# Block 2's up projections as seven block products instead of eight

## The chip, the cores and the metric

The kernel runs on one core of a Trainium2 chip. The metric is the device time of one execution in microseconds (us); the median of three runs of the kernel before is 3358.54 us (3357.44 to 3358.71).

## The reference

The reference is two decoder stacks of depth 2 in float32, one behind the other, over 512 tokens of width 1024. Block 1 (with 16 meta tokens ahead, so 528) has a mixer and a convolved gated feed-forward in each layer. Block 2 has, in each of its two layers, a feed-forward, a mixer (differential attention in layer 0, a gated MLP in layer 1) and another feed-forward. The change is in the four feed-forwards of block 2:

```
def _swiglu_ffn(x, w_gate_up, w_down):
    g, u = jnp.split(x @ w_gate_up, 2, axis=-1)
    return (jax.nn.silu(g) * u) @ w_down

h = h + 0.5 * ffn(rmsnorm(h, g1))
h = h + mixer(rmsnorm(h, g))
h = h + 0.5 * ffn(rmsnorm(h, g2))
```

Here x is 512 x 1024, w_gate_up 1024 x 5632 (2816 gate and 2816 value columns) and w_down 2816 x 1024.

## The kernel before

Features lie on partitions and tokens in columns. A float32 product is made of three passes in the matrix type float32r: each operand is split into a high and a low part of 12 bits, and high x high, high x low and low x high are added in PSUM. So each 128 x 128 block of weights is met by three matmuls (function unit, all issued by the helper mm at L192), in block 2 of 512 columns, in block 1 of 264 or 258 columns (528 or 516 tokens in two PSUM banks). Every matmul instruction comes with a weight load of its own.

Weights come through class WStream in the order of their use. A unit is one column tile of an output, 128 x 1024 floats (512 KB). SP loads units ahead into three raw tiles (L110); each half of a unit (512 columns) is split by ScalarE, which copies it to whi (L124), and VectorE, which subtracts that from the raw half for wlo (L125). There are four buffers for split halves, so the split runs three halves ahead of the matmuls.

A feed-forward of block 2 (ffn2, L534) goes through 22 feature tiles in three groups (FGROUPS: 6, 8, 8). For each feature tile there is a gate unit and a value unit, each of 8 x 3 = 24 matmuls; VectorE multiplies each result by 1/rms (yg, yv, L161), ScalarE applies Silu, VectorE multiplies the two, and the product is split again into ghi (ScalarE, L186) and glo (VectorE). The down units of a group come behind the second tile of the next group: for each of the 8 tiles of the stream h one unit of 6 or 8 tiles x 3 matmuls of 512 columns, whose result VectorE adds to h (L170). In the last group each finished h tile is prepared at once for the next projection (prep: xhi on ScalarE, xlo on VectorE, a square and a sum of squares); the norm itself (finish_norm, L291) is computed behind the first unit that follows and multiplies results later, since each token's 1/rms commutes with the product.

The order of instructions on each engine is not the order in which this file writes them: a planner in the compiler, with its own costs, orders each engine's queue, and each engine then works through its queue in that fixed order. Slots and semaphores follow from the tiles' uses. In block 2 GpSimd (POOL) has no work but one memset; SP's queue holds the weight loads, in order.

Of the kernel before, what the change touches and what calls it, by code (L numbers as in the profile page):

```python
# [21 lines left out]
# tokens that the last convolution of block 1 reads, in two even parts  # L22
# [7 lines left out]
FGROUPS = ((0, 6), (6, 14), (14, 22))  # L30
LEVELS = (1, 2, 4, 8, 16, 32, 64)
# [7 lines left out]
# w_in column tiles of block 1 in the order they are worked on  # L39
# [45 lines left out]
class WStream:  # L85
    """Weight units in the order of their use: loaded ahead, then split exactly into two parts of 12 bits, by halves."""

    RAW = 3
    SPLIT = 4
    HALF = 4 * P  # L90

    def __init__(self, nc, pool):
        self.nc, self.pool = nc, pool
        self.items, self.halves = [], []
        self.raw, self.sp = {}, {}
        self.n_dma = self.n_split = self.i = 0

    def add(self, key, ap):
        n = ap.shape[1]
        for a in range(0, n, self.HALF):  # L100
            self.halves.append((len(self.items), a, min(n, a + self.HALF)))
        self.items.append((key, ap, len(self.halves)))

    def _dma(self, upto):
        while self.n_dma < min(upto, len(self.items)):
            ap = self.items[self.n_dma][1]
            t = self.pool.tile([P, 2 * self.HALF], F32, tag="raw", name="wraw", bufs=self.RAW)
            n = ap.shape[1]
            for a, b in ((0, n),) if self.n_dma else ((0, self.HALF), (self.HALF, n)):
                self.nc.sync.dma_start(t[:, a:b], ap[:, a:b])  # L110
            self.raw[self.n_dma] = t
            self.n_dma += 1

    def prime(self, n):
        self._dma(n)

    def _split(self, upto):
        while self.n_split < min(upto, len(self.halves)):
            u, a, b = self.halves[self.n_split]
            self._dma(u + self.RAW)  # L120
            t, n = self.raw[u], b - a
            hi = self.pool.tile([P, self.HALF], F32R, tag="hi", name="whi", bufs=self.SPLIT)
            lo = self.pool.tile([P, self.HALF], F32R, tag="lo", name="wlo", bufs=self.SPLIT)
            self.nc.scalar.activation(out=hi[:, 0:n], in_=t[:, a:b], func=AF.Copy)  # L124
            self.nc.vector.tensor_tensor(lo[:, 0:n], t[:, a:b], hi[:, 0:n].bitcast(F32), ALU.subtract)  # L125
            self.sp[self.n_split] = (hi, lo, n // P)
            self.n_split += 1

    def prepare(self, n):
        self._split(n)  # L130

    def get(self, key):
        """the parts (hi, lo, slabs) of the next unit, one after the other"""
        u = self.halves[self.i][0]
        k, _, end = self.items[u]
        assert k == key, (k, key)
        while self.i < end:
            i = self.i
            self.i += 1
            self._split(i + self.SPLIT - 1)  # L140
            yield self.sp.pop(i)


class Model:
    def __init__(self, tc, io):
        assert set(self.MERGE) == set(range(KD))
        self.tc, self.nc, self.io = tc, tc.nc, io
        self.pending_norm = None
        self.later = []
        self.slabwise = False  # L150
        self.budget = 0.0
        self.table, self.table_load, self.table_users = None, None, []

# [18 lines left out]
    def after(self, later, earlier):  # L172
        """issue order on one engine"""
# [4 lines left out]
    def act(self, out, a, f, **k):  # L178
        """activations keep to the order of their tables, so that a table is loaded once for all that use it in a row"""
# [14 lines left out]
    def split_scaled(self, src, gcol, hi, lo):  # L194
        """hi + lo = src * gcol"""
# [8 lines left out]
    def unit(self, key, x, new=None, ps=None, first=True, final=True):  # L204
        """psum of w^T x over the slabs of a unit, in three passes"""
# [3 lines left out]
        k, last = 0, self.ws.items[self.ws.halves[self.ws.i][0]][1].shape[1] // P - 1  # L209
# [26 lines left out]
    def new_g2(self):  # L236
        """a unit of block 1 in two tiles of the other kind, for when they have nothing else to do"""
        return self.new_s(), self.new_s()

    def new_s(self):  # L240
        return self.psum.tile([P, 512], F32, tag="s", name="s", bufs=4)

    def hv(self, k):
        """the tokens that the present block works on"""
# [24 lines left out]

    def xg(self, k):  # L270
# [25 lines left out]
    def means(self, parts, ones, src):  # L296
        """means over partitions, of both parts that src is split into"""
# [1161 lines left out]
```

## Time and profile before

| what | before |
|---|---|
| median of 3 runs | 3358.54 us |
| profiled execution: span from its first to its last instruction | 3354.3 us |
| runs' median less that span | 4.2 us |
| TensorE (PE) busy | 3335.8 us, 99% |
| weight loads (PEld) busy | 2894.8 us, 86% |
| VectorE (DVE) busy | 1891.4 us, 56% |
| ScalarE (ACT) busy | 1440.1 us, 43% |
| GpSimd (POOL) busy | 15.8 us |
| DMA | 298.24 MB, mean 89 GB/s |

The profiled execution has no time of its own beside its span. A row "A <-B" of a wait says that A sat idle until B was done. PE's busy time is modelled from the starts of pipelined matmuls, so rates are read here from counts in a stretch.

### The profile page before, as it was taken

To read this page: it belongs to the slowest core of one execution; us is meant where nothing else is said; L and a number is where in the kernel's file an instruction comes from. 1 tells how busy PE (TensorE), PEld (TensorE's weight loads), DVE (VectorE), ACT (ScalarE), POOL (GpSimd) and SP (SyncE) were. 2 spreads that over 40 slices of the span, in tenths; PEclk is the share of its full clock that TensorE was granted. 3 is DMA by queue.
4 is the path that set the end of the run, shared out by engine and by line. 5 is a ranking of instruction groups with operands and counts; after the bars stand their busy time and mean duration, and the time that the engine had idled before them with its cause. 6 is when DMAs were issued, how large, how long until landed. Compare 5 with 4: busy or idle time off the path is not lost.

```text
span 3354.3 us, 48141 instructions
## 1 busy us (share of the span) xinstructions
PE 3335.8 (99%) x19462; PEld 2894.8 (86%) x19462; DVE 1891.4 (56%) x3412; ACT 1440.1 (43%) x2531; POOL 15.8 (0%) x41
## 2 busy tenths in 40 slices
PE   8999999999999999999999999999999999999999
PEld 8999999999999998888887778888888888888887
DVE  7766665667665756544446764445444546554443
ACT  5664343456643435332346642324332335343322
POOL 1000000000000000000000000000000000000000
PEclk9999999999999999999999999999999999999999
DMA  3122322322223233233322123333233332223332
GB/s 127 58 64 89 90 93 89 94 76 64 70 89 95 89 95 95 87 102 94 95 88 67 45 85 94 95 95 94 90 100 94 96 118 88 88 89 94 96 96 91
DMA packets 85647, 298.24 MB, mean 89 GB/s; under 512 B 9761, under 2 KB 9761, under 8 KB 85297
## 3 DMA queue, kind: packets, MB, share of 16 engines
q1 hardware_dynamic: 83664, 289.51, 28.0%
q8 instruction: 153, 2.51, 0.3%
q0 software_dynamic: 1328, 3.56, 0.3%
q10 hardware_dynamic: 432, 2.10, 0.2%
q14 instruction: 70, 0.57, 0.1%
HBM read 293.03 MB, written 2.10 MB: 88 GB/s over the span
## 4 chain that ended last, share of the span: by engine, by line
PE 97%; ACT 1%; DVE 1%; DMA 0%; issue 0%; SPq 0%; ACTq 0%
PE g L192 89%; PE s L192 8%; DMA wraw<-w_in 0%; PE s L1182 0%; PE s L1149 0%; ACT L182 0%; DVE am L1169 0%; ACT p L186 0%; PE s L772 0%; PE s L1215 0%; ACT whi L124 0%; DVE wlo L125 0%; PE s L831 0%; ACT rtmp L186 0%; DVE s L161 0%
## 5 line engine op out<-in xcount | busy, mean ns | idle before, releaser
L124 ACT ACTIVATE whi<-wraw 128x512 fp32r<-128x512 f32 x1112 | 691.6, 623 | 1533.8 <-PE g L192 1460.3
L125 DVE TENSOR_TENSOR wlo<-wraw,whi 128x512 fp32r<-128x512 f32 x1112 | 749.2, 675 | 545.6 <-ACT whi L124 523.4
L192 PE MATMUL g<-xhi,whi 128*128 128x512 f32 (+2 forms) x3696 | 1052.6, 332 | 1.0 <-ACT whi L124 1.0
L192 PE MATMUL g<-xlo,whi 128*128 128x512 f32 (+2 forms) x3696 | 1047.1, 331 | 0.0
L192 PE MATMUL g<-xhi,wlo 128*128 128x512 f32 (+2 forms) x3696 | 1046.3, 331 | 0.2 <-DVE wlo L125 0.2
L192 PEld LDWEIGHTS g<-xhi,whi 128*128 128x128 f32 x3696 | 627.0, 189 | 72.6 <-ACT whi L124 1.2
L192 PEld LDWEIGHTS g<-xhi,wlo 128*128 128x128 f32 x3696 | 626.7, 189 | 65.9 <-DVE wlo L125 0.6
L192 PEld LDWEIGHTS g<-xlo,whi 128*128 128x128 f32 x3696 | 624.3, 189 | 66.7
L192 PE MATMUL g<-glo,whi 128*128 128x512 f32 (+1 forms) x1360 | 469.7, 366 | 0.1
L192 PE MATMUL g<-ghi,whi 128*128 128x512 f32 (+1 forms) x1360 | 469.8, 367 | 0.0
L192 PE MATMUL g<-ghi,wlo 128*128 128x512 f32 (+1 forms) x1360 | 469.7, 367 | 0.0
L192 PEld LDWEIGHTS g<-glo,whi 128*128 128x128 f32 x1360 | 244.0, 188 | 45.8 <-DVE glo L161 0.5
L192 PEld LDWEIGHTS g<-ghi,whi 128*128 128x128 f32 x1360 | 244.0, 188 | 45.3 <-ACT ghi L186 0.2
L192 PEld LDWEIGHTS g<-ghi,wlo 128*128 128x128 f32 x1360 | 243.8, 188 | 45.5
L161 DVE TENSOR_TENSOR yv<-g,rstd 128x512 f32<-128x512 f32 x88 | 60.9, 692 | 132.7 <-PE g L192 132.7
L170 DVE SCALAR_TENSOR_TENSOR h<-g,h 128x512 f32<-128x512 f32 x96 | 66.4, 692 | 120.6 <-PE g L192 120.6
L161 DVE TENSOR_TENSOR yg<-g,rstd 128x512 f32<-128x512 f32 x88 | 60.9, 692 | 130.0 <-PE g L192 129.9
L161 DVE TENSOR_TENSOR h<-g,h 128x512 f32<-128x512 f32 (+2 forms) x84 | 58.4, 697 | 92.8 <-PE g L192 92.8
L186 ACT ACTIVATE ghi<-yv 128x512 fp32r<-128x512 f32 x88 | 55.5, 631 | 121.4 <-DVE yv L161 121.4
L192 PE MATMUL g<-whi,xhi 128*128 128x512 f32 x256 | 102.6, 401 | 0.0
L192 PE MATMUL g<-whi,xlo 128*128 128x512 f32 x256 | 101.3, 396 | 0.0
L192 PE MATMUL g<-wlo,xhi 128*128 128x512 f32 x256 | 101.2, 397 | 0.0
(322 smaller groups left out, 3038.5 us busy)
## 6 DMA issues: line engine op xcount, KB each, us to landing
wraw<-w_up SPq DMA_DIRECT2D x88, 512.0 KB, 3.5
wraw<-w2a_up SPq DMA_DIRECT2D x88, 512.0 KB, 3.5
wraw<-w2b_up SPq DMA_DIRECT2D x88, 512.0 KB, 3.5
wraw<-w_in SPq DMA_DIRECT2D x51, 512.0 KB, 3.5
wraw<-w_down SPq DMA_DIRECT2D x32, 512.0 KB, 3.5
wraw<-w2a_down SPq DMA_DIRECT2D x32, 512.0 KB, 3.5
wraw<-w2b_down SPq DMA_DIRECT2D x32, 512.0 KB, 3.5
wraw<-wa_in SPq DMA_DIRECT2D x24, 512.0 KB, 3.5
```

The source lines that it names most:

```text
L124: self.nc.scalar.activation(out=hi[:, 0:n], in_=t[:, a:b], func=AF.Copy)
L125: self.nc.vector.tensor_tensor(lo[:, 0:n], t[:, a:b], hi[:, 0:n].bitcast(F32), ALU.subtract)
L161: self.nc.vector.tensor_tensor(out, a, b, op)
L170: self.nc.vector.scalar_tensor_tensor(out=out, in0=a, scalar=s, in1=b, op0=op0, op1=op1)
L186: i = self.nc.scalar.activation(out=out, in_=a, func=f, **k)
L192: self.nc.tensor.matmul(out, lhsT, rhs, start=start, stop=stop, **k)
```

## The change

The up projection of a feed-forward is cut into 11 pairs of feature tiles. For a pair, the weights are four blocks of 128 x 1024 floats: two feature tiles (f) by two halves of the 1024 inputs (h), each block holding gate and value side by side; the host lays them out so (_quads). The operand x is cut in four too: two halves of the inputs by two halves of the tokens (256 each). The 2 x 2 block product is formed with seven products of blocks instead of eight, in the form with seven sums of weight blocks and operands computed beforehand and the results combined afterwards. Each of the seven steps is 2 (gate, value) x 4 x 3 = 24 matmuls of 256 columns.

Seven weight blocks are split per pair (1024 columns at a time instead of 512). Four of them are sums. Two are made by DMA: SP loads one block, and GpSimd's queue then adds the second onto it in SBUF (accum_op). The other two are made by VectorE from raw tiles in place. There are 7 raw tiles and 4 buffers of split blocks during a feed-forward of block 2, and 3 and 2 otherwise.

Three PSUM chains of two banks (a, b, c) take the steps' results. ScalarE copies three intermediate results out (ev), VectorE subtracts them from later ones; the rest is as before (1/rms, Silu, product, split), with wider instructions. Down units of 6, 6, 6 and 4 tiles (PGROUPS) instead of 6, 8, 8; those of a group are interleaved with the steps of the next group's first pair, and two PSUM buffers are left for them.

Where a feed-forward follows, the h tiles are finished in the order 0, 4, 1, 5, ... (PAIRED), and prep_pair makes the sums and splits of the operand (prep_first for tiles 0 to 3, prep_second for 4 to 7). This holds for the end of block 1, the attention's and the gated MLP's output projections, and the last group of layer 0's second feed-forward; in front of a mixer prep is as before. Temporary tiles of the other stages are moved into tiles that the operand uses too.

```
+PGROUPS = ((0, 3), (3, 6), (6, 9), (9, 11))
...
+    def add_pair(self, key, quad, stage):
+        st = {}
+        def get(n, i):
+            if n not in st:
+                st[n] = self.item([quad[j] for j in i] if isinstance(i, tuple) else quad[i], stage)
+            return st[n]
+        def step(n):
+            k = key + (n,)
+            if n == 0:
+                self.part(k, get("11", 0), 1024, 0, (), True)
+            elif n == 1:
+                self.part(k, get("s", (1, 2)), 1024, 0, (), True)
+            elif n == 2:
+                self.part(k, st["11"], 1024, 0, ((st["11"], st["11"], st["s"]),), True)
+            elif n == 3:
+                self.part(k, get("12", 3), 1024, 0, (), True)
+            elif n == 4:
+                self.part(k, get("21", (1, 0)), 1024, 0, (), True)
+            elif n == 5:
+                self.part(k, st["12"], 1024, 0, ((st["12"], st["12"], st["11"]),), True)
+            else:
+                self.part(k, get("22", 2), 1024, 0, (), True)
+        return step
...
+            if isinstance(ap, list):
+                self.nc.sync.dma_start(self.raws[s], ap[0])
+                for b in ap[1:]:
+                    self.nc.gpsimd.dma_start(self.raws[s], b, accum_op=ALU.add)
+            else:
...
+        for o, x, y in sums:
+            self.nc.vector.tensor_tensor(self._tile(o), self._tile(x), self._tile(y), ALU.add)
+            for t in (o, x, y):
+                self._drop(t)
+        c = (hs[0] % 2) * self.HALF
+        hi = self.his[hs[0] // 2][:, c:c + n]
+        self.nc.scalar.activation(out=hi, in_=self._tile(src)[:, a:a + n], func=AF.Copy)
...
+    def _ahead(self):
+        while True:
+            more = self._hi()
+            while self.n_lo < self.n_hi and (not self.parts[self.n_lo][5] or self.n_lo < self.n_hi - 1):
+                self._lo()
+                more = True
+            if not more:
+                return
...
+    STEPS = ((0, "a", True), (1, "c", True), (4, "a", False), (2, "b", True), (5, "a", False), (3, "c", False),
+             (6, "a", False))
...
+    def prep_first(self, k, g, ng):
+        n = self.T // 2
+        a, b = self.hv(k)[:, 0:n], self.hv(k)[:, n:2 * n]
+        if k == 0:
+            self.tx = {}
+        self.tx[k] = [self.shared(3 * k + i, F32R) for i in range(3)]
+        self.dt = self.shared(12, name="dt")
+        d = self.dt[:, 0:n]
+        self.tt(d, a, b, ALU.subtract)
+        self.act(self.slot(k, 0), a, AF.Copy, scale=ng)
+        self.act(self.slot(k, 1), d, AF.Copy, scale=g)
+        self.stt(self.slot(k, 0, True), a, ng, self.slot(k, 0).bitcast(F32), ALU.mult, ALU.subtract)
+        self.stt(self.slot(k, 1, True), d, g, self.slot(k, 1).bitcast(F32), ALU.mult, ALU.subtract)
+    def prep_second(self, k, g1, g2):
+        n = self.T // 2
+        b1, h2, d, t4 = self.hv(k)[:, n:2 * n], self.hv(k + 4), self.dt[:, 0:n], self.dt[:, n:2 * n]
+        b2, t = (self.np.tile([P, T1], F32, tag=t, name="ops", bufs=1)[:, 0:2 * n] for t in ("nx", "nw"))
+        self.act(b2, h2, AF.Copy, scale=g2)
+        self.stt(t[:, 0:n], d, g1, b2[:, n:2 * n], ALU.mult, ALU.add)
+        self.stt(t[:, n:2 * n], b1, g1, b2[:, n:2 * n], ALU.mult, ALU.subtract)
+        self.tt(t4, b2[:, 0:n], t[:, 0:n], ALU.subtract)
+        for v, f in ((lambda lo: self.slots(k, 4, lo), t), (lambda lo: self.slots(k, 2, lo), b2), (lambda lo: self.slot(k, 6, lo), t4)):
+            self.act(v(False), f, AF.Copy)
+        for v, f in ((lambda lo: self.slots(k, 4, lo), t), (lambda lo: self.slots(k, 2, lo), b2), (lambda lo: self.slot(k, 6, lo), t4)):
+            self.tt(v(True), f, v(False).bitcast(F32), ALU.subtract)
...
+    def pair_step(self, key, n, ps):
+        s, _, start = self.STEPS[n]
+        w = self.T // 2
+        for wh, wl, _ in self.ws.get(key + (n,)):
+            for e in range(2):
+                o = ps[:, e, 0:w]
+                for k in range(4):
+                    c = slice((4 * e + k) * P, (4 * e + k + 1) * P)
+                    xh, xl = self.slot(k, s), self.slot(k, s, True)
+                    self.mm(o, wh[:, c], xh, start and k == 0, False, skip_group_check=not start)
+                    self.mm(o, wh[:, c], xl, False, False, skip_group_check=not start)
+                    self.mm(o, wl[:, c], xh, False, k == 3, skip_group_check=not start)
+        if n == 3 and self.pending_norm is not None:
+            f, self.pending_norm = self.pending_norm, None
+            f()
+        elif self.later:
+            self.later.pop(0)()
...
+    def pair_seq(self):
+        seq = []
+        for gi, (a, b) in enumerate(PGROUPS):
+            for p in range(a, b):
+                late = list(PAIRED) if gi and p == a else []
+                for n in range(7):
+                    seq.append(("step", p, n))
+                    if n and late:
+                        seq.append(("down", gi - 1, late.pop(0)))
+                seq += [("down", gi - 1, m) for m in late]
+        return seq + [("down", len(PGROUPS) - 1, m) for m in PAIRED]
...
     def ffn2(self, l, which, nextg):
         tc, nc = self.tc, self.nc
         key = (1, l, which)
+        w = T2 // 2
+        self.n_s = 2
+        with tc.tile_pool(name="psf", bufs=1, space=PSUM, reuse_waits="tile") as self.psum, \
+                tc.tile_pool(name="ffn2", bufs=1, reuse_waits="tile") as fp:
+            ghi = [fp.tile([P, 2, T2], F32R, name=f"ghi{i}") for i in range(4)]
+            glo = [fp.tile([P, 2, T2], F32R, name=f"glo{i}") for i in range(4)]
+            ev = [fp.tile([P, 2, w], F32, name=f"ev{i}") for i in range(3)]
+            ys = [fp.tile([P, 2, 2, T2], F32, name=f"y{i}") for i in range(2)]
+            self.ws.open_stage(key, fp, 4, 2)
+            chain = {c: self.psum.tile([P, 2, 512], F32, name="chain" + c) for c in "acb"}
+            r = self.rstd[:, 0:T2]
+            def each(t):
+                return t.rearrange("p (e n) -> p e n", e=1).to_broadcast([P, 2, t.shape[1]])
+            for what, n, m in self.pair_seq():
+                if what == "step":
+                    y = ys[n % 2]
+                    a, b, c = (chain[i][:, :, 0:w] for i in "abc")
+                    self.pair_step(key + ("pair", n), m, chain[self.STEPS[m][1]])
+                    if m < 3:
+                        self.act(ev[m], (a, c, a)[m], AF.Copy)
+                    elif m == 3:
+                        self.tt(y[:, :, 0, 0:w], b, ev[0], ALU.subtract)
+                    elif m == 4:
+                        self.tt(y[:, :, 1, w:], a, ev[1], ALU.subtract)
+                        self.tt(y[:, :, 1, w:], y[:, :, 1, w:], each(r[:, w:]), ALU.mult)
+                    elif m == 5:
+                        self.tt(y[:, :, 0, w:], c, ev[2], ALU.subtract)
+                        self.tt(y[:, :, 0, :], y[:, :, 0, :], each(r), ALU.mult)
+                        self.act(y[:, 0, 0, :], y[:, 0, 0, :], AF.Silu)
+                    else:
+                        self.tt(y[:, :, 1, 0:w], a, each(r[:, 0:w]), ALU.mult)
+                        self.act(y[:, 0, 1, :], y[:, 0, 1, :], AF.Silu)
+                        for f in range(2):
+                            self.tt(y[:, 1, f, :], y[:, 0, f, :], y[:, 1, f, :], ALU.mult)
+                            self.split(y[:, 1, f, :], ghi[n % 4][:, f, :], glo[n % 4][:, f, :])
+                        chain["a"], chain["b"] = chain["b"], chain["a"]
                 else:
+                    p0, p1 = PGROUPS[n]
+                    x = lambda k: (ghi[(p0 + k // 2) % 4][:, k % 2, :], glo[(p0 + k // 2) % 4][:, k % 2, :])
+                    ps = self.unit(key + ("down", n, m), x, self.new_d)
+                    hm = self.hv(m)
+                    self.stt(hm, ps, 0.5, hm, ALU.mult, ALU.add)
+                    if n == len(PGROUPS) - 1:
+                        if nextg is None:
+                            nc.sync.dma_start(self.io["out"][m], hm)
+                        elif which == 2:
+                            self.prep_pair(m, nextg)
+                        else:
...
+def _quads(w):
+    n = w.shape[1] // 512
+    t = _tiles(w).reshape(2, n, 2, P, 2, 512)
+    return np.stack([t[:, :, f, :, h].transpose(1, 2, 0, 3).reshape(n, P, D) for f, h in ((0, 0), (1, 0), (1, 1), (0, 1))], 1)
```

## Rows read from the trace of the kernel before

**Rows 1.** The page: span, busy time of the engines, chain that ended last by engine.

```profile
span 3354.3 us, 48141 instructions
PE 3335.8 (99%) x19462; PEld 2894.8 (86%) x19462; DVE 1891.4 (56%) x3412; ACT 1440.1 (43%) x2531; POOL 15.8 (0%) x41
...
PE 97%; ACT 1%; DVE 1%; DMA 0%; issue 0%; SPq 0%; ACTq 0%
```

**Rows 2.** Windows: busy us and instructions per engine, granted clock, DMA share, GB/s.

```profile
core 0: us, PE busy (x) PEld busy (x) DVE busy (x) ACT busy (x) POOL busy (x), PEclk, DMA share, GB/s
...
970.00:1030.00 60.00, 60.00 (x499) 60.00 (x499) 43.57 (x65) 28.56 (x43) 0.00 (x0) 1.00 0.28 87
2100.00:2250.00 150.00, 150.00 (x647) 121.38 (x647) 65.02 (x99) 46.10 (x73) 0.00 (x0) 1.00 0.31 95
1947.00:1957.00 10.00, 9.32 (x41) 7.21 (x39) 9.93 (x17) 8.06 (x15) 0.00 (x0) 1.00 0.39 107
2290.00:2330.00 40.00, 40.00 (x173) 32.25 (x172) 23.55 (x36) 18.12 (x30) 0.00 (x0) 1.00 0.30 92
```

**Rows 3.** Groups by line and shape: busy us, mean ns | idle before.

```profile
L125 DVE TENSOR_TENSOR wlo<-wraw,whi 128x512 fp32r<-128x512 f32 x1064 | 729.1, 686 | 545.6 <-ACT whi L124 523.4 <-PE s L192 8.7 <-PE g L192 8.2
L124 ACT ACTIVATE whi<-wraw 128x512 fp32r<-128x512 f32 x1064 | 671.6, 632 | 1484.4 <-PE g L192 1414.0 <-PE s L192 33.0 <-issue 17.6
...
L170 DVE SCALAR_TENSOR_TENSOR xlo<-h,cols,xhi 128x512 fp32r<-128x512 f32 x40 | 30.0, 751 | 6.5 <-ACT xhi L186 6.5
...
L124 ACT ACTIVATE whi<-wraw 128x256 fp32r<-128x256 f32 x48 | 20.0, 417 | 49.3 <-PE g L192 46.3 <-DVE wlo L125 3.0
L125 DVE TENSOR_TENSOR wlo<-wraw,whi 128x256 fp32r<-128x256 f32 x48 | 20.0, 417 | 0.0
...
L170 DVE SCALAR_TENSOR_TENSOR p<-p,az,p 128x256 f32<-128x256 f32 x8 | 3.8, 480 | 0.1
...
L161 DVE TENSOR_TENSOR wT<-wT,tri 128x1024 f32<-128x1024 f32 x1 | 1.2, 1224 | 4.8 <-DMA wT<-g_ws 4.8
```

**Rows 4.** Timeline of VectorE at 2338 us: start, duration, instruction.

```profile
2338.65 0.69 DVE L161 TENSOR_TENSOR nw<-nw,nx 128x512 f32<-128x512 f32 x1 [3.10 <-ACT nw L186]
2339.26 0.68 DVE L125 TENSOR_TENSOR wlo<-wraw,whi 128x512 fp32r<-128x512 f32 x1
2339.86 0.68 DVE L170 SCALAR_TENSOR_TENSOR rstd<-nw,rstd 128x512 f32<-128x512 f32 x1
```

**Rows 5.** Timeline of a value unit's end at 2005 us, TensorE, VectorE, ScalarE.

```profile
2005.30 0.40 PE L192 MATMUL g<-xhi,whi 128*128 128x512 f32 x1
...
2005.50 0.69 DVE L161 TENSOR_TENSOR yv<-g,rstd 128x512 f32<-128x512 f32 x1 [1.61 <-PE g L192]
...
2007.43 0.63 ACT L186 ACTIVATE ghi<-yv 128x512 fp32r<-128x512 f32 x1 [1.46 <-DVE yv L161]
...
2008.09 0.69 DVE L161 TENSOR_TENSOR glo<-yv,ghi 128x512 fp32r<-128x512 f32 x1 [0.70 <-ACT ghi L186]
```

**Rows 6.** DMA: the weight queue, issues by tile (us to landing), issue on GpSimd.

```profile
q1 hardware_dynamic: 83664, 289.51, 28.0%
...
wraw<-w2a_up SPq DMA_DIRECT2D x88, 512.0 KB, 3.5
...
rope<-rope POOLq DMA_DIRECT2D x4, 264.0 KB, 5.4
...
L927 POOL DMA_DIRECT2D rope<-rope x4 | 2.3, 572 | 0.0
```

**Rows 7.** Timeline of VectorE at 1341 us, behind the first norm of block 2.

```profile
1341.53 0.68 DVE L161 TENSOR_TENSOR ssq<-s,rstd 128x512 f32<-128x512 f32 x1
...
1343.99 3.40 DVE L170 SCALAR_TENSOR_TENSOR h<-h,cols,rstd 128x512 f32<-128x512 f32 x5
1347.35 0.69 DVE L161 TENSOR_TENSOR nw<-nw,nx 128x512 f32<-128x512 f32 x1
```

More of the change, by code (lines that the diff above doesn't have):

```diff
@@ L88 @@
     RAW = 3
-    SPLIT = 4
+    SPLIT = 2
     HALF = 4 * P
     def __init__(self, nc, pool):
[L93 to L98, printed above, removed]
-        n = ap.shape[1]
[L100 to L127, printed above, removed]
@@ L129, in prepare @@
-    def prepare(self, n):
-        self._split(n)
-    def get(self, key):
[L134 to L137, printed above, removed]
+        self.nc = nc
+        self.raws = [pool.tile([P, 1024], F32, name=f"wraw{i}") for i in range(self.RAW)]
+        self.his = [pool.tile([P, 1024], F32R, name=f"whi{i}") for i in range(self.SPLIT)]
+        self.los = [pool.tile([P, 1024], F32R, name=f"wlo{i}") for i in range(self.SPLIT)]
@@ new lines, in __init__, with item, part @@
+        self.items, self.parts = [], []
+        self.slot_of, self.taken = {}, set()
+        self.half_of, self.held = {}, {}
+        self.age = 0
+        self.used_at = {}
+        self.n_load = self.n_hi = self.n_lo = self.i = 0
+        self.stage = None
+    def item(self, ap, stage=None):
+        self.items.append([ap, stage, 0])
+        return len(self.items) - 1
+    def part(self, key, src, n, a=0, sums=(), wide=False):
+        for o, x, y in sums:
+            for t in (o, x, y):
+                self.items[t][2] += 1
+        self.items[src][2] += 2
+        self.parts.append((key, src, a, n, sums, wide))
@@ new lines, in add, with slabs @@
+    def add(self, key, ap, stage=None, wide=False):
+        n = ap.shape[1]
+        t = self.item(ap, stage)
+        for a in range(0, n, n if wide else self.HALF):
+            self.part(key, t, n if wide else min(n - a, self.HALF), a, (), wide)
+    def slabs(self, key):
+        n, i = 0, self.i
+        while i < len(self.parts) and self.parts[i][0] == key:
+            n += self.parts[i][3] // P
+            i += 1
+        return n
+    def add_pair(self, key, quad, stage):
[21 more added lines that the diff above has]
+        return step
@@ new lines, in open_stage, with close_stage @@
+    def open_stage(self, stage, pool, raws, splits):
+        self.stage = stage
+        self.raws += [pool.tile([P, 1024], F32, name=f"wraw{i + self.RAW}") for i in range(raws)]
+        self.his += [pool.tile([P, 1024], F32R, name=f"whi{i + self.SPLIT}") for i in range(splits)]
+        self.los += [pool.tile([P, 1024], F32R, name=f"wlo{i + self.SPLIT}") for i in range(splits)]
+        self._ahead()
+    def close_stage(self):
+        assert all(s < self.RAW for s in self.taken) and all(h < 2 * self.SPLIT for h in self.held)
+        del self.raws[self.RAW:], self.his[self.SPLIT:], self.los[self.SPLIT:]
+        self.stage = None
@@ new lines, in _oldest, with _load @@
+    def _oldest(self, free):
+        return min(free, key=lambda x: self.used_at.get(x, -1))
+    def _load(self, upto=None):
+        while self.n_load < min(len(self.items), upto or len(self.items)):
+            ap, stage, _ = self.items[self.n_load]
+            own = stage is not None and stage == self.stage
+            free = [s for s in range(len(self.raws)) if s not in self.taken and (own or s < self.RAW)]
+            if not free:
+                return
+            extra = [s for s in free if s >= self.RAW]
+            s = min(extra or free, key=lambda x: self.used_at.get(("r", x), -1))
+            self.taken.add(s)
+            self.slot_of[self.n_load] = s
+            if isinstance(ap, list):
[3 more added lines that the diff above has]
+            else:
+                n = ap.shape[1]
+                t = self.raws[s][:, 0:n]
+                for a, b in ((0, n),) if self.n_load else ((0, self.HALF), (self.HALF, n)):
+                    self.nc.sync.dma_start(t[:, a:b], ap[:, a:b])
+            self.n_load += 1
@@ L149, in __init__ @@
         self.later = []
+        self.n_s = 4
         self.slabwise = False
@@ L334, in units @@
                             ws.add((1, l, kind, g, kp), io["wa_in"][2 * n + g, kp])
-                for half, order in enumerate((AOUT_ORDER, range(KD))):
+                for half, order in enumerate((AOUT_ORDER, PAIRED)):
                     for m in order:
```

239 lines of the change are left out of this document (164 added, 75 removed).

## The prediction

> **What bounds the kernel now.** I read the page's shares and its chain first, then windows of single stages, then the groups by shape, last the timelines at the seams. TensorE is busy for 3335.8 of 3354.3 us and holds 97% of the chain that ended last [rows 1]: only fewer or shorter matmuls help, as long as nothing else becomes late. The reader is to see in the windows that this holds inside the stages: in 2100 to 2250 (up and down units of block 2's feed-forward) TensorE is busy throughout, VectorE 65.0 of 150 us; the exception is 1947 to 1957, the attention's last projection, where VectorE is busy 9.93 of 10 us already [rows 2].
>
> **What is removed: one matmul column in eight.** Before, two feature tiles take 2 x 2 x 8 x 3 = 96 matmuls of 512 columns, and with 11 pairs in 4 feed-forwards 4224. After, 7 x 24 = 168 of 256 columns, in all 7392. A 512-column matmul takes 150 us / 647 = 231.8 ns. No row has 256 columns; the nearest has 258, in block 1's second layer, each matmul with its own weight load as here: 60 us / 499 = 120.2 ns [rows 2], more than half of 231.8. So 4224 x 0.2318 = 979.1 us become 7392 x 0.1202 = 888.5: **90.6 us less**, where the columns alone would give 122. Bounds: with two columns fewer at the slope between the rows, (231.8 - 120.2) / 254 = 0.44 ns each, 119.3 ns and 97 us less; with one matmul fewer in the 60 us, 120.5 ns and 88, say 85. I take 120.2, since weight loads are then busy for the whole window, so that the slope need not go on. The granted clock is 1.00 in all these rows, the 2.4 GHz level. The down units keep their matmuls.
>
> The Trainium skill, "TensorE: Matmul & The Clock Gate", section "Back-to-back issue gap", gives columns / 2.4 GHz + 2.5 ns, 216 and 109 ns here, and adds that in a stream of weight load and matmul both set the spacing. By the formula the change would save 911 - 807 = 104 us; the trace's 231.8 and 120.2 lie 16 and 11 ns above it and side with the second half, so the sum goes by the rows.
>
> **What is added on VectorE and ScalarE.** A VectorE instruction of 512 columns takes 0.69 us, of 256 0.42 and of 1024 1.22 (0.48 and 0.75 with a column factor, at 256 and 512) [rows 3]; back to back the next one starts 0.61 us after one of 0.69 [rows 4], so I count 0.61, 0.34, 1.14 and, with the factor, 0.40 and 0.67. Per pair VectorE had 8 weight splits and 8 other instructions, 16 x 0.61 = 9.8 us in 22.2 of TensorE. Now 7 splits and 2 sums of 1024, 9 x 1.14 = 10.3, and for the results 9 x 0.61 + 1.14 = 6.6: 16.9 us beside 168 x 0.1202 = 20.2. ScalarE, by the same reasoning from 0.42 and 0.63 us, goes from 6.4 to about 10.4. Both fit, VectorE at 84%, in the 8 of 11 pairs that have no down units between their steps; in the other three 33 us of down units give room.
>
> **What comes onto the path at the seams.**
> (a) Last down units. Their last feature tile comes from the pair's last step. From the end of a product to VectorE's first instruction 0.2 us pass, a handover to ScalarE costs 0.03 [rows 5]; product times 1/rms, Silu, product, high, low: 0.2 + 0.69 + 0.63 + 0.69 + 0.63 + 0.69 + four handovers = 3.7 us. These units now have 4 tiles, so it is needed after 3 x 3 matmuls and one more, 2.3 us: 1.4 us late, 4 times, **6 us** (to 10 if VectorE is behind). Before, 7 tiles (4.9 us) covered it.
> (b) prep_pair. For tiles m and m + 4 VectorE has 2 additions to h, 2 sums of squares, 2 weight halves (6 x 0.61), 4 instructions of 256 with a factor (1.6), two of 256 (0.68) and 2 x 0.61 + 0.34 for the low parts: 7.5 us, where 5.0 were. Two units of 8 tiles take 11.1 us on TensorE and cover it (end of block 1, gated MLP). Units of 4 tiles take 5.6: behind the attention and between the layers VectorE ends 4 x 1.9 = 8 us late. It also has three splits and a sum for the first steps (4.6), waits for ScalarE between (some 3), and the first two steps (5.8) cover part: **10 us** each, 20 in all (13 to 28). That VectorE had no reserve there is the third of the windows [rows 2]; the plain prep between layer and mixer (2290 to 2330) has it at 23.6 of 40.
> (c) Openings. A feed-forward starts with three raw tiles until the stage before has left the others. Its second block is an adding one: 3.5 us to land [rows 6], then as long again, against two splits ahead: **2 us** each, 8 in all (0 to 16).
> (d) Pair after pair. At 84% VectorE's order matters. In the order of the file, the last step's results come behind a split and a sum of the next pair: they start 1.35 us late (0.2 + 1.75 + 1.14 + 1.14 - 2.89), take 4.7 with two waits for ScalarE, and the split for the next pair's third step is ready at 7.25 us where TensorE wants it at 6.0: 1.2 us, in the 4 pairs of each feed-forward that have no down units at that seam, 16 x 1.2 = 19 us. But the planner's order is not the file's: the five updates of h that belong behind five later units stand in one row ahead of the norm's next instruction [rows 7]. Between 0 and 19 I take **10**.
> The norm's 6 us behind the fourth step are needed only by the fifth step's result, of which TensorE needs the subtraction alone, so I cost it at nothing; if the file's order held there, 3 us a feed-forward.
>
> **What is added on the DMA.** The queue moves 289.5 MB in 28.0% of 3354 us [rows 6], so a block of 512 KB occupies the engines for 1.70 us. A pair loads 7 blocks instead of 4, two of them adding. No row shows an adding transfer. At least 1.70 us, since the same bytes are read; the far end is the slowest transfer from GpSimd's queue, 5.4 us for 264 KB, so 10.8. I take twice the plain one, 3.4, the nearest row with a second stream read: 5 x 1.7 + 2 x 3.4 = 15.3 us per pair beside 20.2, hidden. GpSimd's issue takes 0.57 us, with nothing else queued there. A raw tile comes free six steps (17 us) or more before its split; load, issue and adding take 3.5 + 0.6 + 3.5 to 11 = 8 to 15. Behind a load that waits stand all later ones on SP, as before.
>
> The Trainium skill, "Collectives: The Full Stack", section "Stop ④ — SDMA + CCE: where bytes move and the add happens", holds that the transfer engine's addition comes free as the bytes stream. By that a pair would need 7 x 1.7 = 11.9 us; no run here shows it yet, and the sum is the same.
>
> **Sum.** 90.6 - 6 - 20 - 8 - 10 = 46.6 us less: span 3354.3 - 46.6 = 3307.7. The runs' median lies 4.2 above the profiled span, so **3312 us**.
>
> **Rivals.**
> 1. *Everything hides* but (a): 90.6 - 6 = 85, 3274 us. For it: the averages of every engine and the planner's freedom. Against: (b) is work beyond TensorE's time, whatever the order.
> 2. *VectorE's fixed queue sets the pace.* The seams at their far ends, 10 + 28 + 16 + 19, and 12 for the norm: 85 us back, gain 5, 3353 us; spread 3335 to 3375. For it: 84%, with a lookahead of three steps. Against: rows 7.
> 3. *The adding transfers become the bound; slower than before.* In the 32 pairs without down units a pair's transfers need 8.5 + 2t. From t = 5.9 us they exceed 20.2, and from 32 x 2 x (t - 5.9) = 46.6, so t = 6.6, the change loses. At 8 us it is 3312 + 138 = 3450, at 10.8 3630. For it: GpSimd's queue is the slowest per byte in the rows. Against: those were small transfers at the start, beside others.
> 4. *The change doesn't do what it says*: 256 columns not at half the time. The row with 258 speaks against it; it is in the bounds of the first term.
>
> **How the numbers follow.** Forecast 0.55 (own range 3285 to 3335), rival 1 0.12, rival 2 0.20, rival 3 0.13. Faster by over 0.2% (6.7 us, about what a measurement of this kernel can tell from no change): 0.55 + 0.12 + 0.08 of rival 2 = 0.75; within it 0.05; slower 0.07 + 0.13 = 0.20. The range 3266 to 3375 leaves out rival 3 and some 0.06 at the ends.
>
> **What would show it.** Right: 7392 matmuls of 256 columns at about 120 ns in windows of pairs alone; VectorE near 17 us per 20 us there; idle TensorE of about 10 us ahead of the feed-forwards behind the attention and between the layers, ended by the operand's low parts; 1 to 2 us at each last down group; no wait of VectorE's sums or ScalarE's copies for raw tiles. Wrong: waits for raw tiles that end with a DMA (rival 3), TensorE waiting in every pair for wlo, whi or ev (rival 2), or matmuls of 256 columns well off 120 ns.

## The result, and the profile after

The kernel after takes 3301.49 us (median of 4 runs, 3299.57 to 3303.84), the kernel before on the same chip 3357.99 (3355.39 to 3358.71): a ratio of 0.9834, 95% interval 0.9821 to 0.9848, 56.5 us faster. The forecast was 3312, 46.5 us. The likeliest case came about; the terms of its sum did not come out as sized, and their errors nearly cancel, which is luck.

The page of the kernel after: span, busy time and instruction count of each engine; DMA queues (packets, MB, share of 16 engines); issues from GpSimd's queue (KB, us to landing).

```profile
span 3300.3 us, 55223 instructions
PE 3241.5 (98%) x22630; PEld 2985.0 (90%) x22630; DVE 2251.4 (68%) x3626; ACT 1607.9 (49%) x2619; POOL 91.7 (3%) x129
...
q1 hardware_dynamic: 94608, 312.58, 31.0%
q0 software_dynamic: 14000, 49.70, 8.7%
...
wraw<-w2a_up POOLq DMA_DIRECT2D x44, 512.0 KB, 6.8
```

TensorE's busy time fell by 94.3 us [rows 1], its idle time (span less busy) rose from 18.5 to 58.8. The matmuls themselves are seen in windows of the kernel after; the first two lie in pairs without down units, the others at the end of the attention.

```profile
core 0: us, PE busy (x) PEld busy (x) DVE busy (x) ACT busy (x) POOL busy (x), PEclk, DMA share, GB/s
...
1985.00:2025.00 40.00, 40.00 (x341) 39.96 (x340) 36.05 (x41) 26.09 (x34) 2.59 (x3) 1.00 0.72 179
...
2559.74:2574.94 15.20, 15.20 (x132) 15.20 (x131) 12.31 (x14) 7.90 (x10) 0.86 (x1) 1.00 0.63 181
...
1955.00:1960.00 5.00, 0.00 (x0) 0.00 (x0) 2.21 (x5) 0.40 (x2) 0.86 (x1) 0.75 1.02 286
...
1965.00:1970.00 5.00, 1.62 (x6) 1.36 (x6) 5.00 (x12) 4.16 (x8) 0.86 (x1) 0.50 0.63 104
1970.00:1975.00 5.00, 2.00 (x8) 1.87 (x9) 5.00 (x8) 1.42 (x3) 0.00 (x0) 0.50 0.01 2
1975.00:1980.00 5.00, 5.00 (x33) 5.00 (x32) 4.72 (x6) 2.60 (x3) 0.00 (x0) 0.70 0.37 105
```

In these pairs TensorE is never idle: 341 matmuls of 256 columns in 40 us, 117.3 ns each, where 120.2 was taken [rows 2]. VectorE is at 36.05 of 40 there and 12.31 of 15.20 later (90% and 81%; forecast 84%). The adding transfers occupy the engines for 8.7% of 3300 us less the 0.3% that this queue had before, 277 us in 88, so 3.15 us each where 3.4 was estimated.

Behind the attention it looks otherwise. From 1955 to 1960 TensorE does nothing, ScalarE works 0.40 and VectorE 2.21 of 5 us, while the DMA engines are full (1.02). TensorE's granted clock falls while it stands: it is 0.50, the 1.2 GHz level, when TensorE resumes, and still 0.70 on average from 1975 to 1980, where TensorE is busy throughout. The timelines of that seam (start, duration, engine, line, instruction, idle time ahead of it and what ended it):

```profile
1952.12 0.86 POOL L199 DMA_DIRECT2D wraw<-w2b_up  x1 [322.55 <-ACT xhi L342]
...
1954.91 0.49 ACT L342 ACTIVATE xhi<-dt,cols 128x256 fp32r<-128x256 f32 x1
1961.34 1.06 ACT L248 ACTIVATE whi<-wraw 128x1024 fp32r<-128x1024 f32 x1 [5.94 <-DMA wraw<-w2b_up]
1962.31 0.71 ACT L342 ACTIVATE ops<-h,cols 128x512 f32<-128x512 f32 x1
...
1956.52 0.69 DVE L317 TENSOR_TENSOR h<-g,h 128x512 f32<-128x512 f32 x1
1963.05 0.48 DVE L326 SCALAR_TENSOR_TENSOR ops<-dt,cols,ops 128x256 f32<-128x256 f32 x1 [5.83 <-ACT ops L342]
...
1967.28 0.69 DVE L317 TENSOR_TENSOR h<-s,h 128x512 f32<-128x512 f32 x1
...
1968.11 0.55 PE L348 MATMUL chaina<-xhi,whi 128*128 128x256 f32 x1 [13.34 <-DVE h L317]
...
1973.01 0.80 PE L348 MATMUL s<-nsplit,ones 128*128 128x512 f32 x1 [3.27 <-ACT nsplit L342]
```

Read it from the bottom. TensorE's first matmul of the feed-forward waits 13.34 us for VectorE's addition to h at 1967.28, the last reader of the attention's PSUM tiles. That addition stands in VectorE's queue behind 4.2 us of the operand's preparation, which waits for ScalarE's `ops` (5.83 us). And `ops` stands in ScalarE's queue behind `whi` of step 1's weights, the first adding block, which waits 5.94 us for the transfer that GpSimd issued at 1952.12 and that took 9.2 us to land, beside five plain loads issued from 1950.03 to 1951.83. So a transfer that was costed as hidden holds up work that does not need it.

### The profile page after: what moved, and what is told of

It is laid out like the page before. It is cut to its first block, busy times and chain, and to the rows that moved or that the text cites. A ratio compares the mean times of both kernels' runs of the same rounds, so it can differ in the third digit from the quotient of the medians.

```text
span 3300.3 us, 55223 instructions
## 1 busy us (share of the span) xinstructions
PE 3241.5 (98%) x22630; PEld 2985.0 (90%) x22630; DVE 2251.4 (68%) x3626; ACT 1607.9 (49%) x2619; POOL 91.7 (3%) x129
## 5 line engine op out<-in xcount | busy, mean ns | idle before, releaser
L248 ACT ACTIVATE whi<-wraw 128x512 fp32r<-128x512 f32 (+2 forms) x1004 | 781.0, 780 | 1353.6 <-PE g L348 652.0
L259 DVE TENSOR_TENSOR wlo<-wraw,whi 128x512 fp32r<-128x512 f32 (+2 forms) x1004 | 872.8, 873 | 369.5 <-ACT whi L248 349.2
L348 PE MATMUL g<-xhi,whi 128*128 128x264 f32 (+2 forms) x2288 | 500.9, 295 | 1.6 <-ACT whi L248 1.6
L348 PE MATMUL g<-xhi,wlo 128*128 128x264 f32 (+2 forms) x2288 | 494.3, 292 | 0.2 <-DVE wlo L259 0.2
L348 PE MATMUL g<-xlo,whi 128*128 128x264 f32 (+2 forms) x2288 | 492.8, 292 | 0.0
L348 PEld LDWEIGHTS g<-xhi,whi 128*128 128x128 f32 x2288 | 362.4, 190 | 9.0 <-ACT whi L248 1.8
L348 PEld LDWEIGHTS g<-xhi,wlo 128*128 128x128 f32 x2288 | 362.3, 190 | 5.9 <-DVE wlo L259 0.4
L348 PE MATMUL s<-ghi,wlo 128*128 128x512 f32 x704 | 277.4, 395 | 5.8 <-DVE wlo L259 5.8
L348 PE MATMUL s<-ghi,whi 128*128 128x512 f32 x704 | 277.8, 395 | 2.5 <-ACT ghi L342 1.7
L348 PE MATMUL s<-glo,whi 128*128 128x512 f32 x704 | 277.3, 395 | 0.0
```

Of the source, the lines that this page charges most:

```text
L248: self.nc.scalar.activation(out=hi, in_=self._tile(src)[:, a:a + n], func=AF.Copy)
L259: self.nc.vector.tensor_tensor(lo, self._tile(src)[:, a:a + n], hi.bitcast(F32), ALU.subtract)
L348: self.nc.tensor.matmul(out, lhsT, rhs, start=start, stop=stop, **k)
```

## The experiments

The theory: TensorE sets the pace of pairs, at 117 to 118 ns per matmul; what is lost is lost at the seams, part of it to VectorE's preparation of the operand, as predicted, and part to ScalarE's fixed queue behind an adding transfer. The rivals: the seam is VectorE's alone; or the adding transfers cost in every pair; or VectorE does. Times are medians, the kernel before ran at 3357.5 to 3357.8 beside them.

**1. All sums on VectorE.**

```
-    self.part(k, get("s", (1, 2)), 1024, 0, (), True)
+    x, y = get("s", 1), get("s+", 2)
+    self.part(k, x, 1024, 0, ((x, x, y),), True)
```

Step 4 is changed likewise.

> All four weight sums on VectorE: the two adding transfers of a pair become two plain loads and a VectorE sum of 1024 columns each (88 more sums of 1.14 us). Theory A (the adding transfers are hidden, and what they are worth is VectorE's time): VectorE then needs 16.9 + 2 x 1.14 = 19.2 us per pair where TensorE needs 168 x 0.118 = 19.8, so its order decides and TensorE waits in the pairs without down units: 0.3 to 1.4 us in each of 32, 3310 to 3345 us, my value 3320 against 3301.5 for the kernel after. Theory B (VectorE has reserve enough and the adding transfers' latency is what costs at the openings): 3290 to 3301, with no TensorE waits inside pairs.

3303.54 us, ratio 0.9836 (0.9823 to 0.985): no difference from the kernel after that can be measured. TensorE's waits from the first pair on, in this kernel:

```profile
engine line waited for: us in total, times, longest us
PE chaina L350 <- DVE h L319: 6.4, 1, 6.4
PE s L350 <- DVE wlo L261: 5.8, 1, 5.8
PE s L1505 <- DVE p L328: 4.8, 1, 4.8
PE s L350 <- ACT nsplit L344: 4.4, 1, 4.4
PE chainb L350 <- DVE y L319: 2.4, 4, 1.1
PE chaina L350 <- DVE y L319: 2.3, 2, 1.9
PE chainc L350 <- ACT whi L250: 2.2, 2, 1.5
PE chaina L350 <- ACT ev L344: 1.9, 4, 0.7
PE chainb L350 <- ACT ev L344: 1.9, 2, 1.5
```

Both theories hold in part. Waits inside pairs (y, ev, whi, without those of the openings) come to 9 us, against 2.6 in the kernel after: VectorE's order begins to show, at the lower edge of what A had. The seam behind the attention falls from 13.3 + 3.3 to 6.4 + 4.4 + 0.7 and the first opening from 3.8 to 1.1 (B). The two cancel: the adding transfers as a whole buy nothing against sums on VectorE. (TensorE's busy time at full clock also rose, by 5 us. Its ends are modelled, so waits of a tenth of a microsecond or so would hide there; this was not taken apart.)

**2. The second block left out.**

```
-    for b in ap[1:]:
-        self.nc.gpsimd.dma_start(self.raws[s], b, accum_op=ALU.add)
```

> The second block of the two adding sums is left out (S and C are then one plain block each; this changes the numbers that the up projections give). Nothing else differs: 5 + 2 plain loads of a block become 7 per pair without an add. Theory A (at the attention's end ScalarE stands still behind the copy of the first adding block, and its queue holds up the operand's preparation): TensorE's idle of 13.3 us at that seam falls to 5 to 8, the first feed-forward's opening loses 2 to 4 us, steady pairs are unchanged: 3288 to 3295 us. Theory B (the seam is VectorE's own work for the operand's sums and splits): 13.3 stays above 11, 3298 to 3302. Theory C (the adding transfers set the pace of pairs): below 3270.

3290.09 us, ratio 0.98 (0.9786 to 0.9813), 11.4 us less than the kernel after. The 13.3 is 7.3, and the 3.8 us of the first opening are 0.9. Theory A, and C is out: steady pairs had nothing to give back. So the price of the adding transfers is 11.4 us, against plain loads without any addition, and what remains of the seam, 7.3 + 3.3, is not theirs.

**3. Step 1's sum on VectorE in first pairs alone.** The edit of experiment 1 for step 1, under `if key[-1] == 0`.

> Only the first pair of each of the four feed-forwards makes its first weight sum (step 1) on VectorE from two plain loads; the other 40 pairs are as in the kernel after. Theory A (ScalarE behind an adding transfer of 9 us at the attention's end): the two plain loads land earlier, the seam's idle of 13.3 us falls to 6 to 9 and the total to 3293 to 3298. Theory B (VectorE's work bounds the seams): a sum of 1.14 us more stands in VectorE's queue at four seams, 3302 to 3306, and the seam's idle is 13 to 15.

3311.6 us, ratio 0.9864 (0.985 to 0.9877): 10 us slower, neither theory. The seam did fall, to 6.4 + 4.4 + 0.7, as in A. But other waits came: 6.0 and 3.5 us for ev and 3.6 for whi, at openings that had no such wait. ScalarE in the first feed-forward:

```profile
1344.89 0.58 ACT L346 ACTIVATE ev<-chainc 128x512 f32<-128x512 f32 x1
1352.29 2.95 ACT L252 ACTIVATE whi<-wraw 128x1024 fp32r<-128x1024 f32 x3 [6.81 <-DMA wraw<-w2a_up]
1355.14 0.57 ACT L346 ACTIVATE ev<-chaina 128x512 f32<-128x512 f32 x1
...
1355.77 0.58 PE L352 MATMUL chaina<-tx,whi 128*128 128x256 f32 x1 [6.03 <-ACT ev L346]
```

It is the same mechanism at the next adding block: `ev`, which frees TensorE's chain, stands behind the copy of a block that has not landed. TensorE's idle time is 5.7 us more than in the kernel after, since the seam gave back 5.0; another 6.8 us are lost to a lower granted clock.

**4. The kernel before with its 512 columns cut in two.**

```
+    if key[0] == 1 and key[3] in ("gate", "val"):
+        for q in (slice(0, 256), slice(256, 512)):
+            self.mm(o[:, q], ww, xx[:, q], start=a, stop=b, skip_group_check=True)
+        continue
     self.mm(o, ww, xx[:, c], start=a, stop=b)
```

> The kernel before with each matmul of 512 columns in the up units of block 2's feed-forwards cut into two of 256 columns with the same weights: 4224 become 8448, the same products and the same number of columns. Theory A (a 256-column matmul with its own weight load takes 118 to 120 ns against 231.8 for 512): 8448 x 0.118 to 0.1202 less 979.1 = 18 to 36 us slower, 3376 to 3394, my value 3385. Theory B (the time goes by columns, 256 at half of 231.8): no change, 3355 to 3361. Theory C (the second matmul needs no new weight load and runs at columns / 2.4 GHz, 107 ns): up to 50 us faster.

3367.54 us, ratio 1.0032 (1.002 to 1.0043). Both halves start a sum of their own in one PSUM tile, and the up projections' numbers differ; only the time is read. 10.05 us over 4224 cuts is 2.4 ns a cut: (231.8 + 2.4) / 2 = 117.1 ns per matmul of 256 columns. The time lies between A and B, nearer to B: half the columns take very nearly half the time, though each half has a weight load of its own. The 120.2 ns of [rows 2] did not carry over.

**5. Two more adding transfers per pair.**

```
-    for b in ap[1:]:
+    for b in 2 * ap[1:]:
```

> GpSimd's queue adds the second block twice, so a pair has four adding transfers instead of two (S and C then hold one block twice; this changes the numbers that the up projections give). Theory A (an adding transfer occupies the 16 DMA engines 3.15 us, worked out from the share of GpSimd's queue): a pair's transfers need 5 x 1.7 + 4 x 3.15 = 21.1 us where TensorE needs 168 x 0.118 = 19.8; in the 32 pairs without down units 1.3 us each, 42 us, and some 7 us more at the openings: 3330 to 3370. Theory B (the addition is free, an adding transfer costs as a plain one, 1.7): 15.3 us per pair, only the openings pay: 3301 to 3312.

3352.06 us, ratio 0.9981 (0.9972 to 0.999): 50.6 us more, inside A's range, but not for A's reason. The windows of one feed-forward's first pairs:

```profile
core 0: us, PE busy (x) PEld busy (x) DVE busy (x) ACT busy (x) POOL busy (x), PEclk, DMA share, GB/s
...
1340.00:1480.00 140.00, 128.34 (x882) 120.51 (x882) 104.89 (x127) 66.79 (x88) 18.14 (x21) 0.94 0.77 189
1480.00:1680.00 200.00, 198.45 (x1393) 185.00 (x1393) 141.09 (x161) 86.77 (x111) 18.12 (x21) 1.00 0.68 171
```

Over these stretches the engines are not full (0.77, then 0.68), and behind the first few pairs TensorE hardly waits, so A's 1.3 us in each pair did not come. The waits stand at the openings, with a lower granted clock behind them (0.94). A plain load and two additions, one after the other, take 5.3 + 7.5 + 7.5 us to land here (medians). Whether the openings pay for this latency or for engines that are nearly full just there (0.87 and 1.00 in the first two stretches of 10 us) was not separated. B is refuted: an added block occupies the engines for 3.0 us (16.1% of 3346 us, less 10, in 176).

**6. Both sums on VectorE in first pairs alone.** Steps 1 and 4 as in experiment 1, under `if key[-1] == 0`.

> Both sums of the first pair of each feed-forward (steps 1 and 4) on VectorE from plain loads, the other 40 pairs as in the kernel after. Theory A (the waits at the openings stand behind adding transfers in ScalarE's fixed queue; in the run with step 1's sum alone on VectorE they moved to the next adding block): TensorE idles at the attention's end 11.6 us as with all sums on VectorE, instead of 16.6, at the first feed-forward 1 instead of 3.8, and no waits for ev remain: 3291 to 3297. Theory B (the extra plain load holds a raw tile longer, and that is what cost 10 us in that run): 3306 to 3314 again, with the waits now at the second pair's first adding block.

3293.12 us, ratio 0.9808 (0.9792 to 0.9824), 8.4 us less than the kernel after: theory A. The waits at the attention's end are 6.45 + 4.43 + 0.71, at the first feed-forward 1.04; one wait of 0.8 for ev stays, and between the layers one of 2.9 for whi stands where 0.3 was. With experiment 3 this settles it: it was not the raw tile held longer, but the next adding block ahead of `ev`.

**7. Sums of squares on GpSimd**, on top of 6, in prep_pair alone.

```
-    self.tt(self.ssq[:, 0:T], self.ssq[:, 0:T], sq[:, 0:T], ALU.add)
+    self.nc.gpsimd.tensor_tensor(self.ssq[:, 0:T], self.ssq[:, 0:T], sq[:, 0:T], ALU.add)
```

> As the kernel with the first pair's sums on VectorE, and the sums of squares of prep_pair (7 additions of 512 columns at each of three seams) on GpSimd instead of VectorE. Theory A (what is left of the seam behind the attention is VectorE's own work, 6.4 us ahead of the first matmul and 4.4 ahead of the norm's): VectorE is relieved of 7 x 0.61 = 4.3 us, the two waits fall to 4 to 8 in sum, 3 to 6 us faster than that kernel. Theory B (GpSimd's additions take over 1.5 us each or slow VectorE's next to them, and the norm waits for them): not faster, and the wait for nsplit grows.

3299.64 us, ratio 0.9825 (0.981 to 0.984): 6.5 us slower than 6, theory B. GpSimd beside VectorE:

```profile
1954.31 2.50 POOL L546 TENSOR_TENSOR ssq<-ssq,sq 128x512 f32<-128x512 f32 x1 [2.63 <-ACT sq L350]
1957.55 1.27 POOL L546 TENSOR_TENSOR ssq<-ssq,sq 128x512 f32<-128x512 f32 x1 [0.74 <-ACT sq L350]
1962.03 7.87 POOL L546 TENSOR_TENSOR ssq<-ssq,sq 128x512 f32<-128x512 f32 x1 [3.22 <-ACT sq L350]
...
1955.60 1.49 DVE L334 SCALAR_TENSOR_TENSOR xlo<-h,ncols,xhi 128x256 fp32r<-128x256 f32 x1
...
1957.61 1.48 DVE L325 TENSOR_TENSOR tx<-dt,tx 128x256 fp32r<-128x256 f32 x1
```

None of the 21 additions runs without VectorE beside it. They take 1.26 to 7.87 us, and VectorE's two instructions take 1.49 and 1.48 us where they took 0.48 and 0.42 in the kernel after. TensorE's wait for h behind the attention rises from 6.45 to 9.11 us; the wait for nsplit falls to 1.07, where B had it grow. The 6.5 us are not all GpSimd's: in the profiled executions TensorE's idle time is 2.4 us more and the time lost to the granted clock 7.0, of which 3.4 in block 1, where nothing was changed. The Trainium skill, "SBUF — State Buffer", section "SBUF: two separate sides", has the two engines share a port pair that one instruction holds to its end; these rows agree.

**8. The last group of three pairs instead of two.**

```
-PGROUPS = ((0, 3), (3, 6), (6, 9), (9, 11))
+PGROUPS = ((0, 2), (2, 5), (5, 8), (8, 11))
```

> The pairs in groups of 2, 3, 3, 3 instead of 3, 3, 3, 2: the last down units of each feed-forward have 6 tiles instead of 4, the same matmuls in all. Theory A (the seam between the layers and the ends of the feed-forwards are late because a unit of 4 tiles, 2.8 us, is shorter than VectorE's work for one h tile, 7.5 us for two): two units of 6 tiles take 8.3 us, the wait of 5.8 us between the layers, the 0.3 + 0.4 before it and the two of 0.9 at the mixers go: 3293 to 3297. Theory B (the wait is the order of VectorE's queue, a weight half behind the operand's preparation, whatever the units' length): 5 to 6 us stay at the seam between the layers, 3298 to 3303.

3285.74 us, ratio 0.9787 (0.9773 to 0.9802): 15.8 us less than the kernel after. The waits that theory A named go, but the gain is twice what A had. The seam between the layers, after and in this kernel:

```profile
2302.00:2321.00 19.00, 12.78 (x52) 9.39 (x51) 18.82 (x40) 12.51 (x25) 0.86 (x1) 0.95 0.28 55
```

```profile
2290.00:2309.00 19.00, 19.00 (x84) 15.49 (x83) 17.20 (x35) 11.77 (x22) 2.59 (x3) 1.00 0.75 201
```

After, VectorE is busy for 18.82 of 19 us and TensorE for 12.78; with units of 6 tiles TensorE is full and VectorE at 17.20. The waits of 5.8, 0.3 and 0.4 there and the two of 0.9 at the mixers are gone, 8.3 us, and the granted clock, 0.50 from 2320 to 2325 in the kernel after, stays at 1.00. In all TensorE's idle time is 10.1 us less and its busy time 4.2, of which 2.2 by the granted clock; smaller waits at the mixers went too. The seam behind the attention is as it was (14.2 + 3.3).

**9. Both mends together.** The edits of 6 and 8.

> Both kinds of seam mended together: the first pair's sums on VectorE, and pairs in groups of 2, 3, 3, 3. Theory A (the two gains, 8.4 and 15.8 us against 3301.5, come from different waits and add): 3274 to 3280. Theory B (they share a wait, at the seam between the layers): 3282 to 3288.

3277.22 us, ratio 0.9763 (0.9748 to 0.9777): 24.3 us less than the kernel after, where the two gains add up to 24.1: theory A. It is the fastest version that computes the whole result, 80.5 us below the kernel before.

**10. The sums of squares left out**, on top of 9: the additions of 7 replaced by nothing in prep_pair.

> As the kernel with both, with the 7 additions to the sum of squares left out at each of three seams (this changes the norm's result). Theory A (what is left of the seam behind the attention is VectorE's own work): 7 x 0.61 = 4.3 us of VectorE's go there, the wait of 6.4 us for the last additions to h falls to 2 to 4 and the norm's wait by some more: 4 to 7 us faster than that kernel, nothing changes at the other two seams. Theory B (the wait hangs on the chain product, addition, copies of ScalarE, not on VectorE's load): the wait stays at 6, under 2 us faster.

3267.29 us, ratio 0.9732 (0.9716 to 0.9748), 9.9 us less than 9: theory A, by more than it had. TensorE's waits behind the attention, first in 9, then here:

```profile
1951.95 0.55 PE L356 MATMUL chaina<-xhi,whi 128*128 128x256 f32 x1 [6.44 <-DVE h L325]
1957.58 0.79 PE L356 MATMUL s<-nsplit,ones 128*128 128x512 f32 x1 [4.43 <-ACT nsplit L350]
```

```profile
1949.02 0.55 PE L356 MATMUL chaina<-xhi,whi 128*128 128x256 f32 x1 [3.57 <-DVE h L325]
1952.13 0.58 PE L356 MATMUL chainc<-xhi,whi 128*128 128x256 f32 x1 [1.91 <-ACT whi L256]
```

With a third wait of 0.7 in each, the seam costs 11.6 us in 9 and 6.2 here: 4.3 us less work on VectorE shorten it by 5.4. A later wait of 1.6 and the 2.6 between the layers go too, which A had not expected. So what was left of the seam hangs on VectorE's load; half of it was shown to go with that load, and the other half was not taken apart.

**11. The norm's first matmul later**, on top of 9: an order edge on TensorE puts it behind the last matmul of step 1.

> As the kernel with both, with the norm's first matmul held behind the second step of the first pair in TensorE's queue. Theory A (the planner put that matmul among the first five of the feed-forward, and TensorE stands behind it for 4.4 us while 40 others could run): the wait for nsplit goes, 3 to 6 us faster than that kernel. Theory B (the matmuls behind it wait for the operand's low parts and the weights at the same time): under 2 us faster, the wait appears at chaina or chainc.

3277.25 us, ratio 0.9764 (0.9749 to 0.9778), no change: theory B. The wait of 4.43 for nsplit is gone, and one of 5.94 for whi stands in its place.

## Why the prediction was right, and where its sum was not

The measured terms are those of the two profiled executions, whose spans differ by 54.0 us. Idle times are the waits of TensorE in the kernel after less those in the kernel before at the same place. The time lost to the granted clock is TensorE's busy time times (1 - granted clock), added up over the span in pieces of 5 us: 6.1 us before, 17.9 after. Each measured term is rounded.

| term, us | forecast | measured |
|---|---|---|
| matmul columns | -90.6 | -106.1 |
| (a) last down units | 6 | 1.7 |
| (b) behind the attention | 10 | 15.9 |
| (b) between the layers | 10 | 6.9 |
| (c) openings (measured: those outside (b)) | 8 | 4.6 |
| (d) pair after pair | 10 | 2.6 |
| mixers and the kernel's start | 0 | 8.0 |
| lower granted clock behind waits | 0 | 11.8 |
| waits under 0.25 us, as the rest | 0 | 0.7 |
| sum | -46.6 | -54.0 |

The columns, (a), the layers' seam, (c) and (d) together came out 33.7 us better than forecast; the attention's seam and the three terms that were at nothing came out 26.4 worse. That the sum is only 7.4 us off is luck in that sense.

**The columns.** Busy time at full clock fell from 3329.7 to 3223.6 us; (979.1 - 106.1) / 7392 is 118.1 ns, and the window from 1985 to 2025 gives 117.3. The term was under-sized by 15.5 us, because the rate was taken from block 1's 258-column matmuls, though the bounds (85 to 97) were meant to hold it. Experiment 4 shows 117.1 in block 2 itself. The step "weight loads are then busy for the whole window, so that the slope need not go on" failed: weight loads are busy throughout here as well (39.96 of 40) and the rate is nearly that of the columns. Why block 1's matmuls take some 2 ns more than their columns would by experiment 4 was not tested. The formula of the Trainium skill weighed there ("TensorE: Matmul & The Clock Gate", "Back-to-back issue gap", 109 ns) lies 8 ns below the trace, not 11.

**(a), the last down units.** The wait for ghi came as forecast, 0.9 us each, but at two of the four feed-forwards alone, those in front of the mixers.

**(d), VectorE in pairs.** 81 to 90% busy where 84% was forecast, and outside the openings no wait of over 0.25 us came of it in 42 of 44 pairs: the 1.2 us that the file's order would have cost a pair did not come, as [rows 7] suggested. Experiment 1 shows how near the edge this is: with 2.3 us more per pair there are ten waits of 0.4 to 1.9 us.

**(b), the seams.** Between the layers the mechanism is the one predicted, units of 4 tiles against VectorE's preparation; experiment 8 removes it. Behind the attention the prediction had VectorE alone. Of the 15.9 us 5 to 6 were the adding transfer's (experiments 6 and 2). Of the other 10 or 11, experiment 10 takes 5.4 away with 4.3 us of VectorE's work; that the remainder is VectorE's too is not shown. Nor were the waits "ended by the operand's low parts": behind the attention they ended with an addition to h that frees PSUM and with ScalarE's `nsplit` for the norm, between the layers with a low half of the weights.

**The adding transfers.** "Hidden" holds for their throughput (3.15 us of the engines against the 3.4 estimated; the median load and addition land in 4.4 + 6.8 = 11 us, in the 8 to 15 forecast), but not for what stands behind them in ScalarE's queue at an opening. The step that failed is "a raw tile comes free six steps (17 us) or more before its split": behind the attention the load was issued at 1947.8, the sum was there 13.5 us later, and ScalarE stood at the block's copy from 1955.4 on, 7.6 us after the load's issue. So the sign "no wait of VectorE's sums or ScalarE's copies for raw tiles" failed as well. The adding transfers cost 11.4 us (experiment 2), and moving all of them to VectorE costs as much (experiment 1). The prediction also weighed the Trainium skill's statement ("Collectives: The Full Stack", "Stop ④ — SDMA + CCE: where bytes move and the add happens") that the addition comes free as the bytes stream, and took from it 1.7 us for an adding block. In engine time that reading is out: 3.0 to 3.15 us for an adding block, 1.7 for a plain one [rows 6]. An adding block also has to read what it adds to, and no run here separates that from the addition itself.

**The clock.** No term stood for it. Behind the long waits the granted clock is 0.50, the 1.2 GHz level, as from 1965 to 1975, and 11.8 us more than before were lost by it: 4.6 at the first opening, 4.3 around the attention's end, 2.8 between the layers. A seam's price is its wait and the slow stretch behind it. With that stretch the openings cost 9.2 us and the layers' seam 9.7, near the 8 and 10 forecast, but the forecast had no clock in it.

**The rivals.** Everything hides (3274): experiment 9 comes near it (3277.2), by other means. VectorE's queue setting the pace (3353) is out by the pairs' full windows. The adding transfers as the bound (from 5.9 us) are out at 3.15; experiment 5 shows that doubling them costs 50.6 us, most of it lost at the openings, with the engines at 0.68 of full in the stretch behind the first of them. What the mixers and the start lose, 8.0 us, stays open: temporary tiles were moved there, but no run tested whether that is the cause.

## What to carry to other kernels

Cost a transfer on the path by what stands behind its first reader in that engine's fixed queue, not by whether the transfer engines have time: at a stage's opening a late block stops work that has nothing to do with it. Where a stage ends with work per tile on VectorE, make the last units on TensorE longer than that work; here regrouping alone gave 15.8 us, more than a quarter of what the whole change gave. And take a matmul's rate for a new width from the same operands cut to that width, which one experiment shows, rather than from another stage.

## What was not expected of the hardware

Halving a matmul of 512 columns costs 2.4 ns, with a weight load for each half (experiment 4). A DMA that adds onto SBUF occupies the engines some 1.8 times as long as a plain one (3.15 us against 1.70 for 512 KB), and lands in 6.8 us where the plain one takes 4.4 beside it. A GpSimd addition of 512 columns beside VectorE took 1.26 to 7.87 us, and single instructions of VectorE next to it over three times as long as otherwise (experiment 7).
